# A low-rank update rewritten with counted semaphores, with a hardware loop on TensorE and other transfer sizes

## The chip, the cores and the metric

The kernel runs on one core of a Trainium2 chip. The metric is the device time of one launch in microseconds; less is better. The kernel before was run three times, 125.34 to 125.68 us, with a median of 125.58 us. One more execution was profiled.

## What is computed

```python
batch, seq, d_model, r = 16, 512, 768, 16
# x: 16 x 512 x 768 float32, A: 768 x 16, B: 16 x 768, scale 0.5
lora = np.matmul(np.matmul(x, A), B)
return (x + scale * lora).astype(np.float32)
```

Each of the 8,192 rows of x is multiplied by A down to 16 numbers and by B up to 768 again, and half of that is added to the row. x comes in once and goes out once in float32, 25.2 MB each way.

## The kernel before

A tile is 128 rows of x, one row to a partition; there are 64 tiles. They are moved in parts and computed in groups of 8, so there are 8 groups, numbered g. PARTS (line 13) gives the tiles of each part: 8, 8, 16, 16, 8, 8. Row by row a part is laid out so that a partition holds consecutive rows, and a transfer moves one contiguous piece for each of 128 partitions. ROOM (line 15) names four buffers; the last two parts use the buffers of the first two again. LOADS (line 17) splits the loads of parts 0 and 2 in halves of 4 and of 8 tiles. `loaded` (line 67) issues them.

All transfers of x go through SyncE's queue, in this order: loads of parts 0 to 3 at once, store of part 0, store of part 1, loads of parts 4 and 5 (each waits until the store that empties its buffer has landed), and the stores of parts 2 to 5, each when the last group of its part is added up (`finished`, line 157). A and B are small and go through ScalarE's queue (lines 89 and 90).

Before the first group, VectorE clears `a_rows` (line 87), turns A (line 98) and copies it into the block-diagonal weights `w_bd` (line 103), then copies B four times into `b_mm` (line 108). GpSimd clears `w_bd`, `b_mm` and `y_bd`.

A group takes these steps. `narrowed` (line 110) casts x to float16, four tiles on ScalarE and four on GpSimd, into one of two buffers `xh`. `turned` (line 116) transposes these in place on VectorE, in two instructions, in 32 x 32 blocks of 4-byte elements, so a pair of float16 values stays together. `projected` (line 123) multiplies by A on TensorE: 24 products into `ps_yt`. `spread` (line 134) scales the result and writes it into the block-diagonal `y_bd`, four instructions on ScalarE. `raised` (line 142) multiplies by B on TensorE, two tiles at a time, four products into one of two buffers `lora_ps`. `added` (line 152) adds these to x in place on VectorE, two tiles at a time, so four instructions a group.

The order on each engine is written out by hand (lines 167 to 194). For group g TensorE does `raised` 0 and 1, a third of `projected` of group g+1, `raised` 2, a third, `raised` 3, a third. VectorE does the two transposes of group g+1 and then the four adds of group g. ScalarE does the cast of group g+2 and then `spread` of group g+1. A framework puts the semaphores in; the program is straight-line code on every engine.

Of the kernel before, what the change touches and what calls it, by code (L numbers as in the profile page):

```python
# [9 lines left out]
MM_DT = mybir.dt.float16  # L10


PARTS = [8, 8, 16, 16, 8, 8]

ROOM = ["a", "b", "c", "d", "a", "b"]

LOADS = {0: [4, 4], 2: [8, 8]}


GROUP = 8  # L20

SUB = 4


@with_exitstack
def kernel(
    ctx: ExitStack,
    tc: tile.TileContext,
    x: bass.AP,
    A: bass.AP,  # L30
    B: bass.AP,
    scale: bass.AP,
    out: bass.AP,
):
    nc = tc.nc
    fp32 = mybir.dt.float32
    P = 128
    Q = 32

    x2 = x.flatten_outer_dims()  # L40
    out2 = out.flatten_outer_dims()
    T, D = x2.shape
    R = A.shape[1]
    NC = D // 64
    NG = sum(PARTS) // GROUP
    assert sum(PARTS) * P == T and NG * GROUP == sum(PARTS)
    sc = float(scale)

    const = ctx.enter_context(tc.tile_pool(name="const", bufs=1))
    xpool = ctx.enter_context(tc.tile_pool(name="xp", bufs=1))  # L50
    ypool = ctx.enter_context(tc.tile_pool(name="yp", bufs=1))
    ps_y = ctx.enter_context(tc.tile_pool(name="ps_y", bufs=2, space=bass.MemoryType.PSUM))
    ps_l = ctx.enter_context(tc.tile_pool(name="ps_l", bufs=2, space=bass.MemoryType.PSUM))

    parts = []
    where = []
    tok = 0
    for i, S in enumerate(PARTS):
        parts.append([None, tok, S])
        where += [(i, s) for s in range(S)]  # L60
        tok += S * P

    def rows(t2, i):
        _, tok0, S = parts[i]
        return t2[ds(tok0, S * P), :].rearrange("(p s) d -> p s d", s=S)

    def loaded(i):
        S = parts[i][2]
        t = xpool.tile([P, S, D], fp32, name=f"x_sb{i}", tag=ROOM[i])
        parts[i][0] = t  # L70
        end = 0
        for w in LOADS.get(i, [S]):
            nc.sync.dma_start(out=t[:, ds(end, w), :], in_=rows(x2, i)[:, ds(end, w), :])
            end += w

    a_rows = const.tile([Q, 64 * R], fp32, name="a_rows")
    a_t = const.tile([Q, 2, R, Q], fp32, name="a_t")
    b_f32 = const.tile([R, D], fp32, name="b_f32")  # L80
    w_bd = const.tile([P, NC, 2, P], MM_DT, name="w_bd")
    b_mm = const.tile([P, D], MM_DT, name="b_mm")
    xh = [const.tile([P, GROUP, D], MM_DT, name=f"xh{i}") for i in range(2)]
    y_bd = [const.tile([P, GROUP, P], MM_DT, name=f"y_bd{i}") for i in range(2)]

    ctx.enter_context(tc.manual_schedule())
    nc.vector.memset(a_rows, 0.0)  # L87
    loaded(0)
    nc.scalar.dma_start(out=b_f32, in_=B)
    nc.scalar.dma_start(out=a_rows[0:NC, :], in_=A.rearrange("(c e) r -> c (e r)", e=64))  # L90
    for i in range(1, 4):
        loaded(i)
    nc.gpsimd.memset(w_bd.rearrange("p c k m -> p (c k m)").bitcast(fp32), 0.0)  # L93
    nc.gpsimd.memset(b_mm.bitcast(fp32), 0.0)  # L94
    for t in y_bd:
        nc.gpsimd.memset(t.rearrange("p s m -> p (s m)").bitcast(fp32), 0.0)  # L96

    nc.vector.transpose(  # L98
        out=a_t.rearrange("i k r c -> i (k r) c"),
        in_=a_rows.rearrange("c (i k r) -> c (k r) i", k=2, r=R),  # L100
    )
    for b in range(P // Q):
        nc.vector.tensor_copy(  # L103
            out=w_bd[ds(b * Q, Q), :, :, ds(b * Q, R)],
            in_=a_t[:, :, :, 0:NC].rearrange("i k r c -> i c k r"),
        )
    for b in range(P // Q):
        nc.vector.tensor_copy(out=b_mm[ds(b * Q, R), :], in_=b_f32)  # L108

    def narrowed(g):  # L110
        for q in range(GROUP // SUB):
            i, s = where[g * GROUP + q * SUB]
            engine = nc.gpsimd.tensor_copy if q % 2 else nc.scalar.copy
            engine(out=xh[g % 2][:, ds(q * SUB, SUB), :], in_=parts[i][0][:, ds(s, SUB), :])  # L114

    def turned(g):
        for q in range(GROUP // SUB):
            v = xh[g % 2][:, ds(q * SUB, SUB), :].bitcast(fp32)
            nc.vector.transpose(out=v, in_=v)  # L119

    y_ps = {}

    def projected(g, steps):
        if g not in y_ps:
            y_ps[g] = ps_y.tile([P, GROUP, Q], fp32, name="ps_yt")
        xv = xh[g % 2].rearrange("p s (c j k) -> p s c j k", c=NC, k=2)
        for m in steps:
            c, k = divmod(m, 2)
            nc.tensor.matmul(  # L129
                y_ps[g], w_bd[:, c, k, :], xv[:, :, c, :, k],  # L130
                start=(m == 0), stop=(m == 2 * NC - 1),
            )

    def spread(g):
        y = y_ps.pop(g)
        for b in range(P // Q):
            q = ds(b * Q, Q)
            nc.scalar.mul(out=y_bd[g % 2][q, :, q], in_=y[q, :, :], mul=sc)  # L138

    lora = {}  # L140

    def raised(g, p):
        t = ps_l.tile([P, 2, D], fp32, name="lora_ps")
        lora[g, p] = t
        for h in range(2):
            lhsT = y_bd[g % 2][:, 2 * p + h, :]
            for n0, w in ((0, 512), (512, 256)) if h == 0 else ((0, 256), (256, 512)):
                nc.tensor.matmul(  # L148
                    t[:, h, ds(n0, w)], lhsT, b_mm[:, ds(n0, w)], start=True, stop=True
                )  # L150

    def added(g, p):
        i, s = where[g * GROUP + 2 * p]
        xs = parts[i][0][:, ds(s, 2), :]
        nc.vector.tensor_tensor(out=xs, in0=xs, in1=lora.pop((g, p)), op=mybir.AluOpType.add)  # L155

    def finished(g):
        i, s = where[g * GROUP + GROUP - 1]
        if s + 1 == PARTS[i]:
            nc.sync.dma_start(out=rows(out2, i), in_=parts[i][0])  # L160
            if i == 1:
                loaded(4)
                loaded(5)

    MMS = 2 * NC
    THIRD = MMS // 3
    narrowed(0)
    narrowed(1)
    turned(0)
    projected(0, range(MMS))  # L170
    spread(0)
    for g in range(NG):
        more = g + 1 < NG
        raised(g, 0)
        raised(g, 1)
        if g + 2 < NG:
            narrowed(g + 2)
        if more:
            turned(g + 1)
        added(g, 0)  # L180
        if more:
            projected(g + 1, range(0, THIRD))
        raised(g, 2)
        added(g, 1)
        if more:
            projected(g + 1, range(THIRD, 2 * THIRD))
        raised(g, 3)
        added(g, 2)
        if more:
            projected(g + 1, range(2 * THIRD, MMS))  # L190
        added(g, 3)
        finished(g)
        if more:
            spread(g + 1)


# [33 lines left out]
```

## Time and profile before

| | us |
|---|---|
| median of three runs | 125.58 |
| the profiled execution | 125.14 |
| its span, first to last instruction | 123.3 |
| VectorE busy | 89.8 |
| TensorE busy (products) | 51.8 |
| ScalarE busy | 35.3 |
| GpSimd busy | 25.1 |

The span is what the profile shows; the 1.8 us between it and the profiled time lie around it. A busy share is a mean over the span, so each engine must be looked at in the stage where it might be last. The profile's page cuts the span into 40 slices of 3.1 us and gives the busy tenths of each engine and of the 16 DMA engines that carry the transfers. Beneath the page's DMA rows the trace keeps a record for each packet, with its queue, its size, its start and its duration; where the text speaks of packet records, it means these.

A transfer that is issued is not under way yet: the DMA engines work through what one queue was given in order of issue. A store that is issued while earlier transfers are still moving costs nothing as long as it is there before the engines run out of work.

### The profile page before, as it was taken

Reading aid. Unit: us, or ns where it says so; the run is one execution under the profiler, and the core shown is the slowest. Engines: PE = TensorE matmul, PEld = TensorE weight load, DVE = VectorE, ACT = ScalarE, POOL = GpSimd, SP = SyncE. Lnnn points to the kernel's source line nnn. Section 1 sums busy time; section 2 is a strip of 40 time slices with the busy share of each in tenths; the row PEclk is TensorE's granted clock in tenths of the full one; section 3 lists DMA queues with packets and bytes.
Section 4 is the critical chain, followed back from the end, with each engine's and each line's share of the span. In section 5 each row is a group of like instructions: output and inputs, shape, how many; then the busy total and the mean of one; then the engine's idle time right before and its main releaser. Section 6 shows DMA issues by size and latency. Waiting matters only on the chain.

```text
span 123.3 us, 854 instructions
## 1 busy us (share of the span) xinstructions
PE 51.8 (42%) x320; PEld 32.3 (26%) x320; DVE 89.8 (73%) x58; ACT 35.3 (29%) x41; POOL 25.1 (20%) x16
## 2 busy tenths in 40 slices
PE   0000001948943844844794594484489432000000
PEld 0000001625622522532462362252246210000000
DVE  2019997826999999999989999999998499000000
ACT  1235007149094040849004084354000400000000
POOL 8101807135080000844000080350000000000000
PEclk9999999999999999999779999999977999555555
DMA  4999999999998897999999999989989989999980
GB/s 73 398 371 466 406 454 414 454 430 391 510 510 383 383 499 335 430 414 454 414 446 422 422 454 507 407 383 494 449 351 478 478 351 446 391 438 438 414 375 32
DMA packets 2075, 50.47 MB, mean 409 GB/s; under 512 B 252, under 2 KB 252, under 8 KB 280
## 3 DMA queue, kind: packets, MB, share of 16 engines
q1 hardware_dynamic: 2016, 50.33, 96.0%
q10 hardware_dynamic: 56, 0.10, 0.4%
q8 instruction: 2, 0.03, 0.1%
q14 instruction: 1, 0.01, 0.0%
HBM read 25.26 MB, written 25.17 MB: 409 GB/s over the span
## 4 chain that ended last, share of the span: by engine, by line
DVE 57%; PE 12%; issue 6%; DMA 5%; ACT 2%; DVEq 1%; ACTq 0%
DVE x_sb L155 31%; DVE xh L119 19%; PE ps_yt L129 8%; DMA a_rows<-in_A_dram 5%; PE lora_ps L148 5%; DVE w_bd L103 3%; ACT y_bd L138 2%; DVE b_mm L108 2%; DVE a_t L98 2%; DVEq L225 1%; DVE a_rows L87 1%; ACTq L225 0%; ACTq L138 0%; DVEq L103 0%; DVEq L98 0%
## 5 line engine op out<-in xcount | busy, mean ns | idle before, releaser
L155 DVE TENSOR_TENSOR x_sb<-x_sb,lora_ps 128x1536 f32<-128x1536 f32 x32 | 54.0, 1741 | 6.2 <-PE lora_ps L148 6.2
L129 PE MATMUL ps_yt<-xh,w_bd 128*128 128x256 f16 x192 | 28.8, 299 | 31.1 <-DVE xh L119 31.1
L148 PE MATMUL lora_ps<-b_mm,y_bd 128*128 128x512 f16 (+1 forms) x128 | 26.1, 338 | 19.7 <-ACT y_bd L138 13.8
L114 POOL CAST xh<-x_sb 128x3072 f16<-128x3072 f32 x8 | 22.2, 2781 | 56.2 <-DMA x_sb<-in_x_dram 49.7
L129 PEld LDWEIGHTS <-w_bd 128*128 128x128 f16 x192 | 20.2, 105 | 39.4 <-issue 33.3
L114 ACT CAST xh<-x_sb 128x3072 f16<-128x3072 f32 x8 | 22.0, 2752 | 23.8 <-DMA x_sb<-in_x_dram 23.7
L119 DVE STREAM_TRANSPOSE xh<-xh 128x1536 f32<-128x1536 f32 x16 | 27.4, 1754 | 1.0 <-ACT xh L114 1.0
L138 ACT ACTIVATE y_bd<-ps_yt 32x256 f16<-32x256 f32 x32 | 12.0, 375 | 35.9 <-PE ps_yt L129 35.3
L148 PEld LDWEIGHTS <-y_bd 128*128 128x128 f16 x128 | 12.1, 100 | 30.6 <-ACT y_bd L138 16.1
L98 DVE STREAM_TRANSPOSE a_t<-a_rows 32x1024 f32<-32x1024 f32 x1 | 1.9, 1931 | 6.9 <-DMA a_rows<-in_A_dram 6.9
L103 DVE CAST w_bd<-a_t 32x384 f16<-32x384 f32 x4 | 4.3, 1087 | 0.1
L108 DVE CAST b_mm<-b_f 16x768 f16<-16x768 f32 x4 | 2.2, 550 | 0.1
L114 ACT ACT_TABLE_LOAD x1 | 1.3, 1283 | 2.5 <-DVE a_rows L87 2.5
L87 DVE MEMSET a_rows<- 32x1024 f32 x1 | 0.9, 912 | 1.0 <-PEq L211 1.0
L93 POOL MEMSET w_bd<- 128x1536 f32 x1 | 1.4, 1379 | 0.3 <-POOLq L211 0.3
L96 POOL MEMSET y_bd<- 128x512 f32 x2 | 1.0, 528 | 0.0
L94 POOL MEMSET b_mm<- 128x384 f32 x1 | 0.4, 418 | 0.0
L211 POOL MEMSET const-float32-0.0<- 128x1 f32 x1 | 0.1, 100 | 0.2 <-issue 0.2
L211 POOL MEMSET const-bfloat16-1.0<- 128x1 bf16 x1 | 0.1, 103 | 0.0
L211 POOL MEMSET const-uint8-127<- 128x1 uint8 x1 | 0.1, 102 | 0.0
L211 POOL MEMSET const-float32-1.0<- 128x1 f32 x1 | 0.1, 100 | 0.0
## 6 DMA issues: line engine op xcount, KB each, us to landing
x_sb<-in_x_dram SPq DMA_DIRECT2D x5, 3072.0 KB, 20.9
out_dram<-x_sb SPq DMA_DIRECT2D x4, 3072.0 KB, 18.5
out_dram<-x_sb SPq DMA_DIRECT2D x2, 6144.0 KB, 24.7
x_sb<-in_x_dram SPq DMA_DIRECT2D x1, 6144.0 KB, 45.6
x_sb<-in_x_dram SPq DMA_DIRECT2D x2, 1536.0 KB, 9.1
b_f<-in_B_dram ACTq DMA_DIRECT2D x1, 48.0 KB, 4.0
a_rows<-in_A_dram ACTq DMA_DIRECT2D x1, 48.0 KB
```

The source lines that it names most:

```text
L87: nc.vector.memset(a_rows, 0.0)
L93: nc.gpsimd.memset(w_bd.rearrange("p c k m -> p (c k m)").bitcast(fp32), 0.0)
L98: nc.vector.transpose(out=a_t.rearrange("i k r c -> i (k r) c"), in_=a_rows.rearrange("c (i k r) -> c (k r) i", k=2, r=R),)
L103: nc.vector.tensor_copy(out=w_bd[ds(b * Q, Q), :, :, ds(b * Q, R)], in_=a_t[:, :, :, 0:NC].rearrange("i k r c -> i c k r"),)
L108: nc.vector.tensor_copy(out=b_mm[ds(b * Q, R), :], in_=b_f32)
L114: engine(out=xh[g % 2][:, ds(q * SUB, SUB), :], in_=parts[i][0][:, ds(s, SUB), :])
L119: nc.vector.transpose(out=v, in_=v)
L129: nc.tensor.matmul(y_ps[g], w_bd[:, c, k, :], xv[:, :, c, :, k], start=(m == 0), stop=(m == 2 * NC - 1),)
L138: nc.scalar.mul(out=y_bd[g % 2][q, :, q], in_=y[q, :, :], mul=sc)
L148: nc.tensor.matmul(t[:, h, ds(n0, w)], lhsT, b_mm[:, ds(n0, w)], start=True, stop=True)
L155: nc.vector.tensor_tensor(out=xs, in0=xs, in1=lora.pop((g, p)), op=mybir.AluOpType.add)
L225: with _tile.TileContext(nc) as tc:
```

## The change

The same steps are kept, with the same instructions on VectorE, ScalarE and GpSimd for each group. What differs:

- PARTS is 2, 6, 8, 16, 16, 16. The first three parts lie side by side in one buffer of 16 tiles, the next two in buffers of their own, and the last part comes into the first buffer again, in two loads of 8 tiles, and goes out in two stores of 8. Loads of 16 tiles are not split. The first cast on ScalarE, tiles 0 to 3, waits for the loads of 2 and of 6 tiles.
- The first reload waits for the stores of parts 0 and 1 together, the second for the store of part 2. Both early stores of parts 0 and 1 wait for group 0.
- Tile buffers and semaphores are allocated by hand. Each engine has a program of its own in a block; entering and leaving the block and the section around it adds instructions. At the end GpSimd waits for the last four stores and clears all semaphores, and then the closing sequence of before follows.
- The four copies into `b_mm` are on ScalarE, ahead of its first cast, and no longer on VectorE.
- ScalarE's order is `spread` of group g, then the cast of group g+2, which puts the same steps in the same sequence as before.
- VectorE has a drain after the four adds of a group, and the drain raises the count that SyncE's stores wait for.
- TensorE runs a hardware loop of four turns, two groups a turn (`h` is 0 and 1). A turn's first part raises the group before, so in the first turn four `raised` steps work on the cleared `y_bd`. What its waits take, they count down again (`take`), so each turn waits for the same values. The last group's four `raised` steps stand behind the loop.

```diff
-PARTS = [8, 8, 16, 16, 8, 8]
-ROOM = ["a", "b", "c", "d", "a", "b"]
-LOADS = {0: [4, 4], 2: [8, 8]}
+PARTS = [2, 6, 8, 16, 16, 16]
+ROOM = [(0, 0), (0, 2), (0, 8), (1, 0), (2, 0), (0, 0)]
...
+    LOADS = [(0, 0, 2), (1, 0, 6), (2, 0, 8), (3, 0, 16), (4, 0, 16), (5, 0, 8), (5, 8, 8)]
...
+    @block.sync
+    def _(e):
+        def store(i, s, n, done):
+            e.wait_ge(s_sum, sums_for(i, s, n))
+            e.dma_start(out=memory(out2, i, s, n), in_=held(i, s, n)).then_inc(done, 16)
+        load(LOADS[0])
+        for ld in LOADS[1:5]:
+            load(ld)
+        store(0, 0, 2, s_out0)
+        store(1, 0, 6, s_out0)
+        store(2, 0, 8, s_out1)
+        e.wait_ge(s_out0, 32)
+        load(LOADS[5])
+        e.wait_ge(s_out1, 16)
+        load(LOADS[6])
+        store(3, 0, 16, s_out)
+        store(4, 0, 16, s_out)
+        store(5, 0, 8, s_out)
+        store(5, 8, 8, s_out)
+    def narrowed(e, copy, done, g, q):
+        t = g * GROUP + q * SUB
+        for s in dict.fromkeys(load_sem(t + k) for k in range(SUB)):
+            e.wait_ge(s, 16)
+        if g >= 2:
+            e.wait_ge(s_y, g - 1)
+        copy(
+            out=xh[g % 2][:, ds(q * SUB, SUB), :], in_=held(*where[t], SUB)
+        ).then_inc(done, 1)
+    @block.scalar
+    def _(e):
+        e.dma_start(out=b_f32, in_=B).then_inc(s_b, 16)
+        e.wait_ge(s_ready, 1)
+        e.dma_start(
+            out=a_rows[0:NC, :], in_=A.rearrange("(c e) r -> c (e r)", e=64)
+        ).then_inc(s_a, 16)
+        e.wait_ge(s_zero, 1)
+        e.wait_ge(s_b, 16)
+        for b in range(NQ):
+            last = e.copy(out=b_mm[ds(b * Q, R), :], in_=b_f32)
+        last.then_inc(s_bm, 1)
...
+        narrowed(e, e.copy, s_nact, 0, 0)
+        narrowed(e, e.copy, s_nact, 1, 0)
+        for g in range(NG):
+            spread(g)
+            if g + 2 < NG:
+                narrowed(e, e.copy, s_nact, g + 2, 0)
+    @block.vector
...
+        turned(0)
+        for g in range(NG):
+            if g + 1 < NG:
+                turned(g + 1)
+            for p in range(PAIRS):
+                xs = held(*where[g * GROUP + 2 * p], 2)
+                e.wait_ge(s_lora, (g + 1) * PAIRS + p + 1)
+                e.tensor_tensor(
+                    out=xs, in0=xs, in1=lora[p % 2], op=mybir.AluOpType.add
+                ).then_inc(s_free, 1)
+            e.drain().then_inc(s_sum, 1)
+    @block.tensor
+    def _(e):
+        def take(s):
+            e.wait_ge(s, 1)
+            e.sem_inc(s, -1)
...
+        def raised(h, p):
+            if p == 0:
+                take(s_spread)
+            take(s_free)
...
+        with e.Fori(0, NG // 2):
+            for h in range(2):
+                raised(1 - h, 0)
+                raised(1 - h, 1)
+                projected(h, range(0, THIRD))
+                raised(1 - h, 2)
+                projected(h, range(THIRD, 2 * THIRD))
+                raised(1 - h, 3)
+                projected(h, range(2 * THIRD, MMS))
+        for p in range(PAIRS):
+            raised(1, p)
+    programs.close()
+    nc.gpsimd.wait_ge(s_out, 4 * 16)
...
+    nc.gpsimd.sem_clear(range(nums[0], nums[0] + len(nums)))
+    section.close()
```

## The prediction

> **What bounds the kernel now.** I read the page first (busy shares, slices, DMA queues), then the windows view for the DMA share stage by stage, then SyncE's queue (when each transfer is issued, what it waited for), and last the order of time on VectorE.
>
> ```profile
> span 123.3 us, 854 instructions
> ...
> PE 51.8 (42%) x320; PEld 32.3 (26%) x320; DVE 89.8 (73%) x58; ACT 35.3 (29%) x41; POOL 25.1 (20%) x16
> ...
> DMA  4999999999998897999999999989989989999980
> ...
> q1 hardware_dynamic: 2016, 50.33, 96.0%
> ...
> q8 instruction: 2, 0.03, 0.1%
> ```
>
> VectorE is the busiest compute engine at 73%, and the chain of waits runs over it. But the DMA row reads 9 in nearly every slice, and the one queue that carries x in and out takes 96.0% of 16 engines' span. The windows view says the same (columns: stretch, length, busy of PE, PEld, DVE, ACT, POOL, clock, DMA share, GB/s):
>
> ```profile
> 34.00:42.00 8.00, 3.94 (x27) 2.61 (x28) 8.00 (x5) 4.25 (x5) 2.75 (x1) 1.00 1.04 449
> ...
> 79.50:94.00 14.50, 9.81 (x60) 6.18 (x60) 14.50 (x9) 3.76 (x5) 2.33 (x1) 0.89 1.01 434
> ...
> 109.00:116.00 7.00, 0.00 (x0) 0.00 (x0) 0.00 (x0) 0.00 (x0) 0.00 (x0) 0.50 1.03 442
> ```
>
> A share of 1 means that all 16 engines are moving data, also after 105 us, when no compute is left. So the span is 1.75 us until the first data packet, 120.4 us of packets, and 1.17 us after the last (122.17). In the trace's packet records a 24,576-byte packet takes 912 ns and a 49,152-byte one 1815: 8 ns a packet plus 0.0368 ns a byte. For 1/16 of 50.33 MB in 112 packets that is 116.5 us; the other 3.9 us are start, small transfers and stragglers. VectorE sets the time only if a transfer is issued after its queue has run empty:
>
> ```profile
> 56.77 0.34 SPq L73 DMA_DIRECT2D x_sb<-in_x_dram  x1
> ...
> 66.10 0.34 SPq L160 DMA_DIRECT2D out_dram<-x_sb  x1
> ...
> 86.05 0.34 SPq L160 DMA_DIRECT2D out_dram<-x_sb  x1
> ...
> 96.71 0.33 SPq L160 DMA_DIRECT2D out_dram<-x_sb  x1
> ...
> 105.15 0.33 SPq L160 DMA_DIRECT2D out_dram<-x_sb  x1
> ```
>
> In the packet records the first engine is through with the work queued ahead of these stores at 76.3, 90.8, 105.3 and 112.6 us. Issue to first packet took 1.0 us for the first load (0.74 to 1.75). So the stores have 9.2, 3.7, 7.6 and 6.4 us to spare; the tightest is the second, part 3 of before.
>
> **The change, part by part.** *Transfers.* The queue still gets 14 transfers of 128 rows, in the same sequence: 48 tiles in, 16 out, 16 in, 16, 16, 8, 8 out. Sizes differ: 2+6 tiles for 4+4 and 16 for 8+8. By 8 ns a packet this is nothing: 14 x 8 packets on each engine in both. The reload's first half now waits for stores 0 and 1 together, 8 tiles, landing when store 0 of before did (56.65), so it is issued at about 56.8 with store 2's 7.3 us of packets as cover; without that cover it costs 1.0 us. Value 0, bounds 0 and 1.0.
>
> *VectorE's start.* Four b_mm copies leave VectorE (15.25, 2.24 us) for ScalarE, which was idle from 3.8 to 8.3. ScalarE's first cast now waits for 8 tiles, as GpSimd's did (11.88), not 4 (8.32).
>
> ```profile
> 8.79 1.93 DVE L98 STREAM_TRANSPOSE a_t<-a_rows 32x1024 f32<-32x1024 f32 x1 [6.87 <-DMA a_rows<-in_A_dram]
> ...
> 15.25 2.24 DVE L108 CAST b_mm<-b_f 16x768 f16<-16x768 f32 x4
> ...
> 28.80 6.75 DVE L155 TENSOR_TENSOR x_sb<-x_sb,lora_ps 128x1536 f32<-128x1536 f32 x4 [3.42 <-PE lora_ps L148]
> ...
> 34.03 2.75 POOL L114 CAST xh<-x_sb 128x3072 f16<-128x3072 f32 x1 [4.69 <-PE ps_yt L129]
> ...
> 38.82 6.71 DVE L155 TENSOR_TENSOR x_sb<-x_sb,lora_ps 128x1536 f32<-128x1536 f32 x4
> ```
>
> The first transposes can start at 15.25 for 17.52, and the first adds at 26.5 for 28.80. If A lands up to 2.3 us later behind the new 6-tile load, that gain is gone. Either way it is lost at group 2: its cast waits for all 16 tiles of part 3, the 32nd tile, which landed at 33.23 by the packet records, where before it needed the 24th (26.59). On ScalarE spread(1) is queued behind that cast. So: cast 33.5 to 36.3, VectorE's two transposes to 39.8 (3.43), adds of group 1 from 39.8 for 38.82. VectorE then runs 1.0 us late at 10.0 us a group (48.79 to 58.77), with the two slow-clock stalls. Group 5's store, 86.05, goes to about 87.1, still 2.7 us ahead of 89.8. Value 0.
>
> *TensorE.* The loop body keeps the order of products; 16 products of zeros run before the first group, while TensorE idled until 21.1. Its separate semaphore steps (51 ns each in the trace, 6 a group, 0.3 us) lie in the 2.0 us it waits for ScalarE each group. The drain after each group's adds comes just ahead of the store's issue and spends some of the 2.7 us. Value 0; without the cover 8 x 0.3 = 2.4 us.
>
> *Instruction fetches.* The row "q8 instruction" is two packets of 16,384 bytes, at 45.50 and 76.45, 1069 and 1099 ns long, each on a DMA engine that also moves x. The packets behind them took 506 and 363 ns longer than 1815, so a fetch sets one engine back 1.5 us. The engine with the first is the last of all, 122.17; without it, 120.6. Next come the one with the second, 121.45, and one that had slow packets but no fetch, 121.34; the rest end between 119.9 and 120.7. [...] One fetch late: that engine ends at 120.2 + 1.5 = 121.7, so -0.45; no fetch, no straggler: -1.5; both fetches, 0.
>
> *Front and end.* No row shows the added steps, so bounds. SyncE has a no-op, a wait for it and a taken branch ahead of its first load: three steps at 65 ns (122.526 to 122.591 in the closing rows) is 0.2; below, 0.1 if two overlap; above, 0.4 at 120 ns each (barrier, 0.536 to 0.656). At the end SyncE's wait for the stores becomes GpSimd's, then a clear of semaphores (96 ns), a hand-over to SyncE and back (33 + 42 ns), four steps at 65: 0.43; below 0.2; above 0.8, the whole closing sequence (122.53 to 123.33) again.
>
> [...]
>
> **The sum**, against the profiled execution: span 123.33 + 0.2 + 0.43 - 0.45 = 123.5; with the 1.8 us around the span (125.14 - 123.33), 125.3. That is 0.2 above the profiled 125.14. The median of the runs is 125.58, 0.44 above the profiled one, so on its scale 125.7.
>
> **The rivals.** *A, the fetches were the price and go.* For it: the last engine to finish is the one with the first fetch. Against it: a third engine ends at 121.34 without any. If none falls in the span and no straggler takes the place: 125.58 + 0.2 + 0.43 - 1.5 = 124.7.
>
> [...]
>
> *C, a store comes late.* If VectorE falls 2.7 us further back by group 5, the DMA queue runs dry at 91 us. For it: the two stalls at the halved clock (61 and 92 us) cost 2 us each, and their place may move. Against: before has 3.7 us to spare there with both in. At 4 us more: 125.58 + 0.2 + 1.3 = 127.1, less what it overlaps with the straggler, 126.6.
>
> **How the numbers follow.** Within 0.3%, or 0.38 us, is about what a measurement of this kernel can tell from no change. Forecast 125.7 at 0.50, own range 125.3 to 125.9; A 0.20; B 0.15; C 0.15. A is faster, B and C slower: 0.20, 0.50, 0.30. The range reaches to A's 124.7 less 0.1, and up past the high ends of front and closing without a gain (125.58 + 0.4 + 0.8 = 126.8) and C to 127.3, leaving out most of B.
>
> **What would show it.** Right: DMA share near 1 from 3 to 121 us, first load issued near 0.95, the last data packet near 121.9, 1.6 us from it to the end, VectorE's second group of adds near 39.8 and its last near 106. Wrong: gaps in the DMA row near 56 or 91 us, more than two packets on the instruction queue, or a first load later than 1.2 us.

## The result, and the profile after

| | before | changed |
|---|---|---|
| median of 18 runs | 125.33 us | 124.83 us |
| profiled execution | 125.14 us | 124.72 us |
| its span | 123.3 us | 122.9 us |

The ratio is 0.9969, with a 95% interval of 0.9954 to 0.9984. Two more series on other chips gave 0.9983 (0.9964 to 1.0001) and 0.9959 (0.9937 to 0.9980). So the change makes the kernel about 0.3% faster, some 0.4 us, where no change was forecast. The page of the changed kernel, in the lines that answer to those shown of before:

```profile
span 122.9 us, 965 instructions
...
PE 54.2 (44%) x336; PEld 32.2 (26%) x336; DVE 85.6 (70%) x54; ACT 38.6 (31%) x45; POOL 25.0 (20%) x16
...
DMA  2999995995997996999999999999899899799990
...
q1 hardware_dynamic: 2016, 50.33, 96.0%
...
q14 instruction: 2, 0.02, 0.0%
```

The transfers fill the span as before. The 5s in the DMA row are a matter of counting: the row and the windows view put a packet's whole time where the packet begins, so that a thin slice stands beside a full one. By the packet records all 16 engines are busy throughout the slices with a 5. The row that is missing is the one to see: there is no "q8 instruction" any more, so no packet of 16,384 bytes fell into this span. It still comes: the packet records have it at 124.01 us, behind the last instruction at 122.9. The two on q14 have 8,192 bytes; before had one of that kind in its span, at 89.1 us. Such a packet takes 0.31 us and the one behind it was 0.1 to 0.5 us over its size; the two engines ended at 121.01 and 121.24, ahead of the last one at 121.45. Now VectorE in order of time, and the one row of ScalarE that it waits for:

```profile
14.53 3.44 DVE L214 STREAM_TRANSPOSE xh<-xh 128x1536 f32<-128x1536 f32 x2 [2.41 <-ACT xh L150]
...
26.59 6.75 DVE L224 TENSOR_TENSOR x_sb<-x_sb,lora_ps 128x1536 f32<-128x1536 f32 x4 [1.38 <-PE lora_ps L255]
36.30 3.44 DVE L214 STREAM_TRANSPOSE xh<-xh 128x1536 f32<-128x1536 f32 x2 [2.96 <-ACT xh L150]
39.66 3.38 DVE L224 TENSOR_TENSOR x_sb<-x_sb,lora_ps 128x1536 f32<-128x1536 f32 x2
```

```profile
33.52 2.75 ACT L150 CAST xh<-x_sb 128x3072 f16<-128x3072 f32 x1 [8.07 <-DMA x_sb<-in_x_dram]
```

The first adds start 2.2 us earlier than before (26.59 for 28.80), and then VectorE waits 2.96 us for ScalarE's cast, which waits for the load of 16 tiles. Group 1's adds start 0.8 us later than before (39.66 for 38.82). SyncE's queue:

```profile
0.94 2.77 SPq L123 DMA_DIRECT2D x_sb<-in_x_dram  x5
33.42 13.67 SPq L127 DMA_DIRECT2D out_dram<-x_sb  x3
55.52 7.93 SPq L123 DMA_DIRECT2D x_sb<-in_x_dram  x2
67.17 38.94 SPq L127 DMA_DIRECT2D out_dram<-x_sb  x4
```

The first load is issued 0.2 us later than before. The last four stores are issued at 67.17, 87.59, 97.80 and 105.78, each 0.6 to 1.5 us later than before and still ahead of the end of the work in the queue.

The stretches of the two profiled executions, by the packet records and the instruction records:

| us | before | changed | difference |
|---|---|---|---|
| span's start to the first load's issue | 0.74 | 0.945 | +0.2 |
| from there to the first packet of x | 1.01 | 1.03 | 0 |
| first to last packet of x | 120.43 | 119.48 | -0.95 |
| last packet to the span's end | 1.16 | 1.50 | +0.34 |

The gain lies in the third row alone, and part of it is given back in the first and the last. What lies around the span is 1.8 us in both of these executions.

### The profile page after: what moved, and what is told of

The parts are those of the page before. It is cut to its first block, busy times and chain, and to the rows that moved or that the text cites. A ratio compares the mean times of both kernels' runs of the same rounds, so it can differ in the third digit from the quotient of the medians.

```text
span 122.9 us, 965 instructions
## 1 busy us (share of the span) xinstructions
PE 54.2 (44%) x336; PEld 32.2 (26%) x336; DVE 85.6 (70%) x54; ACT 38.6 (31%) x45; POOL 25.0 (20%) x16
## 5 line engine op out<-in xcount | busy, mean ns | idle before, releaser
L255 PE MATMUL lora_ps<-b_mm,y_bd 128*128 128x512 f16 (+1 forms) x144 | 31.0, 352 | 37.4 <-PEq L233 37.4
L241 PE MATMUL ps_yt<-xh,w_bd 128*128 128x256 f16 x192 | 27.1, 285 | 11.8 <-PEq L233 11.8
L255 PEld LDWEIGHTS lora_ps<-b_mm,y_bd 128*128 128x128 f16 x144 | 13.3, 103 | 50.6 <-issue 44.8
L241 PEld LDWEIGHTS ps_yt<-xh,w_bd 128*128 128x128 f16 x192 | 18.9, 100 | 20.1 <-issue 14.8
L174 ACT CAST b_mm<-b_f 16x768 f16<-16x768 f32 x4 | 3.3, 829 | 0.0
L204 DVE CAST w_bd<-a_t 32x384 f16<-32x384 f32 x4 | 1.9, 472 | 0.1
```

The source lines that it names most:

```text
L174: last = e.copy(out=b_mm[ds(b * Q, R), :], in_=b_f32)
L204: last = e.tensor_copy(out=w_bd[ds(b * Q, Q), :, :, ds(b * Q, R)], in_=a_t[:, :, :, 0:NC].rearrange("i k r c -> i c k r"),)
L241: last = e.matmul(y_ps[h], w_bd[:, c, k, :], xv[:, :, c, :, k], start=(m == 0), stop=(m == MMS - 1),)
L255: last = e.matmul(t[:, k, ds(n0, w)], y_bd[h][:, 2 * p + k, :], b_mm[:, ds(n0, w)], start=True, stop=True,)
```

## The experiments

Each kernel is the changed one with one edit. Times of single executions scatter by 0.2 to 0.3 us, spans by 0.1 to 0.2, so the mean span of a series is given beside the ratio to the kernel before on the same chip. The changed kernel's mean span was 122.99 (18 executions), 123.05 (12) and 122.90 (8) on three chips; the kernel before had 123.2 to 123.5.

**TensorE's loop written out.**

```diff
-        with e.Fori(0, NG // 2):
+        for _ in range(NG // 2):
```

> The changed kernel with TensorE's loop written out, so that its stream grows from 240 to 751 instructions; nothing else differs. Theory (instruction fetches in the span set single DMA engines back 1.5 us each, and the last engine sets the end): two or three packets of 16,384 bytes appear on the instruction queue inside the span, the engines that carry them end 1.2 to 1.6 us later than their neighbours, and the time is 0.5 to 0.9 us above the changed kernel, so 1.000 to 1.004 of the kernel before. Rival (the gain comes from the new transfer sizes or from VectorE's earlier start): the time stays at 0.997 of the kernel before, whatever is fetched.

Measured: 1.0163 (1.0141 to 1.0185), mean span 124.32. The profile has two packets of 16,384 bytes, at 45.24 and 87.42 us. The engine with the first ended last, at 122.64 us, 2.4 us behind the typical engine; the one with the second ended at 121.43. More came than was expected: 1.3 us in the span, and the time around the span was 2.55 us for 1.8. The rival falls.

The packet records say where the 0.7 us around the span belong: a third packet of 16,384 bytes lies behind the last instruction, at 125.84 us. Five of the profiles have one there (two of the changed kernel, this one, and two of kernels below), and in each the packet's end, counted from the span's start, is the execution's time plus 0.23 to 0.24 us. The time around the span is 1.8 to 2.55 us in these five and 1.8 to 1.9 in the others. This suggests that a fetch behind the span still lengthens the time; no run tests that by itself.

**One fetch late in the span.**

```diff
         for p in range(PAIRS):
             raised(1, p)
+        for _ in range(200):
+            e.wait_ge(s_w, 1)
```

> The changed kernel with 200 waits on a count that is already there, placed behind TensorE's last product; they end about 110 us and nothing waits for them but the barrier that opens long before the last store lands. They only lengthen TensorE's stream by 100 instructions. Theory: one packet of 16,384 bytes on the instruction queue between 103 and 111 us, one DMA engine 1.5 us later than without it, ending near 121.9 to 122.3 against 121.4, and the time up by 0.3 to 0.8 us. Rival (what counts is the number of instructions run, or the loop, not the fetch): no change from the changed kernel within 0.2 us.

Measured: 0.9998 (0.9982 to 1.0015), mean span 123.19. The packet came, at 109.13 us. The price is 0.2 us over the changed kernel's mean span and, by the ratio, 0.2 to 0.5 us over its three series, which were on other chips; the low end of what was expected is not excluded. In the profile the fetch did not set the end: its engine ended at 121.42, ahead of one at 121.67 that had slow packets and no fetch. So a fetch this late matters little, and what it costs is not settled.

**The loop moved by 100 places, first try.**

```diff
         e.wait_ge(s_w, 1)
         e.wait_ge(s_bm, 1)
+        for _ in range(200):
+            e.wait_ge(s_w, 1)
         with e.Fori(0, NG // 2):
```

> The changed kernel with 200 such waits ahead of TensorE's loop, where TensorE idles until 12.5 us anyway. [...]

Measured: 1.019 (1.0137 to 1.0243), but not because the loop had moved. The waits stand behind the wait for the weights, so they ran after it, at 106 ns each, and TensorE began at 23.6 us for 12.5. VectorE came late all the way, and the store of part 4 was issued at 93.29, after the queue had run empty. The windows view shows it (columns as above: DMA share is the last but one):

```profile
84.00:91.00 7.00, 4.53 (x32) 2.78 (x31) 7.00 (x5) 1.87 (x1) 0.41 (x1) 1.00 0.97 421
91.00:94.30 3.30, 1.44 (x12) 0.85 (x11) 3.16 (x3) 1.50 (x4) 0.00 (x0) 1.00 0.64 271
94.30:104.00 9.70, 5.37 (x38) 3.24 (x37) 9.13 (x6) 1.50 (x4) 0.00 (x0) 1.00 0.94 405
```

The share drops to 0.64 between 91.0 and 94.3; counted packet by packet it is 0.22 there, and most engines stood still for 2.1 to 3.1 us. This execution took 128.56 us, more than the quickest two (126.43 and 126.46), so only its gap is used. It is the prediction's rival C, made by hand. One packet of 16,384 bytes came, at 105.76 us, so the loop did not fetch once a turn; but as TensorE ran late, its place was tested again.

**The same, without delaying TensorE.**

```diff
+        for _ in range(180):
+            e.wait_ge(s_spread, 1)
         e.wait_ge(s_w, 1)
         e.wait_ge(s_bm, 1)
```

> The changed kernel with 180 waits on a count that is already there, ahead of TensorE's first wait for the weights, where it idles until 12.5 us: 90 instructions of 106 ns, done near 11 us. They move the loop by 90 places without delaying it. In the run that put such waits behind that wait, TensorE began 11 us late, group 5's store came when the queue had been empty for 3 us, and only one packet of 16,384 bytes fell in the span. Theory: with TensorE on time the queue never runs empty, one or two such packets, 0.9995 to 1.004. [...]

> The same kernel as the one with 90 instructions ahead of TensorE's loop, whose executions fell into two lots, three with spans of 122.9 to 123.2 and nine of 124.4 to 124.9; the one that was profiled was of the lower lot and had a single packet of 16,384 bytes, at 78.4 us. Theory (fetches): an execution of the upper lot has an engine that carries such a packet earlier, before 76 us, or carries two, and ends 1.4 us later for it. Rival (a store comes late): a gap in the DMA row before a store, as where TensorE began 11 us late.

Measured: 1.0056 (1.0027 to 1.0085) and, again, 1.0088 (1.0057 to 1.0119). The first series fell into two lots, three executions with spans up to 123.2 us and nine from 124.4; in the second, one was of the lower lot. The first profile is of the lower lot: one packet of 16,384 bytes at 78.44 us, its engine at 121.49, the span 122.9. The second is of the upper lot: one such packet at 30.92 us, its engine at 123.07, the span 124.4. The ratios lie above the theory's 1.004; the count of packets, one in each profile, is within its one or two. The second page:

```profile
span 124.4 us, 1055 instructions
...
DMA  2999996998899698999999999998997998999960
...
q8 instruction: 1, 0.02, 0.1%
```

By the packet records the engines are busy throughout from 3 to 118 us, so no store came late; what differs is when the one fetch came. It did not come once a turn. But in both profiles it came behind a jump back of the loop: the jump before 30.92 us was at 30.19, and the one before 78.44 was at 74.60, after which TensorE waited until 77.6. So it is not excluded that a jump called for that one fetch.

**One turn written out, three in the loop.**

```diff
-        with e.Fori(0, NG // 2):
+        def turn():
             for h in range(2):
...
+        turn()
+        with e.Fori(0, NG // 2 - 1):
+            turn()
```

> The changed kernel with the first of the loop's four turns written out ahead of a loop of three. TensorE does the same in the same order; its stream grows from 240 to 412 instructions, and what it runs until 60 us is as in the kernel with all four turns written out, where a packet of 16,384 bytes came at 45.2 us. Theory (a fetch in mid-span costs its DMA engine 1.5 us, and 0.6 to 1.2 us more at the turn from loads to stores near 76 us, as the engines with such a fetch showed in the kernel before and in the written-out one): one such packet near 45 us, that engine the last of all, and a span 0.7 to 1.3 us above the changed kernel's 123.0 (mean of 30 executions). Rival (only fetches late in the span or their number count): below 0.3 us.

Measured: 1.0061 (1.0037 to 1.0086), mean span 124.13, 1.1 above the changed kernel's. One packet of 16,384 bytes, at 45.44 us, as in the written-out kernel:

```profile
q8 instruction: 1, 0.02, 0.1%
```

```profile
119.50:121.50 2.00, 0.00 (x0) 0.00 (x0) 0.00 (x0) 0.00 (x0) 0.00 (x0) 0.50 0.20 86
121.50:123.00 1.50, 0.00 (x0) 0.00 (x0) 0.00 (x0) 0.00 (x0) 0.00 (x0) 0.50 0.04 16
```

The windows show what a straggler looks like: for packets that begin between 119.5 and 121.5 us the share is 0.20, and for those that begin later only 0.04, which is less than one engine of 16. That one engine holds up the whole kernel to 122.83; the next ended at 121.41. This is the cleanest dose: the same work in the same order, one fetch in mid-span, and 1.1 us. Expected was 0.7 to 1.3.

The engines with a fetch, each followed through the packet records by linking a packet to the one that ended when it began (a packet of 49,152 bytes takes 1815 ns, one of 24,576 takes 912):

| kernel | fetch at, us | it took, ns | the packet behind it, ns over its size | its packet of 24,576 near 76 us, ns | engine ends at, us |
|---|---|---|---|---|---|
| shifted, again | 30.92 | 1069 | +499 | 2325 | 123.07 |
| written out | 45.24 | 1098 | +469 | 2144 | 122.64 |
| one turn out | 45.44 | 1069 | +499 | 2040 | 122.83 |
| before | 45.50 | 1069 | +506 | 1499 | 122.17 |
| before | 76.45 | 1099 | +363 | 914 | 121.45 |
| shifted | 78.44 | 934 | +400 | 1074 | 121.49 |
| written out | 87.42 | 966 | +378 | 1007 | 121.43 |

A fetch ahead of 76 us costs its engine 1.6 us at once and 0.6 to 1.4 us more at 76. There the queue turns from loads to stores. The other engines finish their last load packet, and the one that is behind has one load packet more than they; the packet that it is moving at that moment, its last but one, is the long one, and the last takes 912 ns again. Not every late engine is late by a fetch: where TensorE began 11 us late, two engines without one in mid-span had a packet of 2158 and 1942 ns there. And engines that are not late lose a little: in the changed kernel's profile the last load packet of each engine took 0.1 to 0.7 us too long, in that of before none of the others did by more than 0.02.

A fetch after 76 us costs 1.3 to 1.5 us and puts its engine where another engine ends in any case: each of these profiles has an engine with six or more packets some 50 to 100 ns too long and no fetch, which ends at 121.3 to 121.4.

**The transfer sizes of before.**

```diff
-PARTS = [2, 6, 8, 16, 16, 16]
+PARTS = [8, 8, 16, 16, 8, 8]
...
+    LOADS = [
+        (0, 0, 4), (0, 4, 4), (1, 0, 8), (2, 0, 8), (2, 8, 8), (3, 0, 16), (4, 0, 8), (5, 0, 8)
+    ]
```

> The changed kernel with the parts, loads and stores of the kernel before (4+4, 8, 8+8, 16 tiles in; 8, 8 out; 8, 8 in; 16, 16, 8, 8 out); the rest as changed. Theory (the sizes do nothing): the same time as the changed kernel within 0.2 us, 0.996 to 0.998 of the kernel before, though group 2's cast starts near 27 instead of 33.5 us and VectorE ends about 1 us earlier. Rival (the sizes gave the gain): back to 1.000 of the kernel before, or above it by the 0.5 us that front and closing cost.

> The changed kernel with the parts, loads and stores of the kernel before, and with the waits of the last group's four raised steps not counted down, so that TensorE's stream is 4 instructions shorter (236). The run with these sizes alone had one packet of 16,384 bytes at 103.7 us, three instructions from TensorE's end, and 0.9995. Theory (fetches, not sizes): with the stream shorter the fetch falls behind the end of the span, and the time is that of the changed kernel, 0.996 to 0.998. If the fetch is still there, 0.999 to 1.000. Rival (the sizes): 0.999 to 1.000 without a fetch in the span.

Measured: 0.9995 (0.9982 to 1.0008), mean span 122.92, and for the shorter stream 0.9983 (0.9968 to 0.9999), mean span 123.21. Both profiles had one late fetch (103.72 and 98.48 us), so the second did not take it away as was meant. By the ratios the first agrees with the rival, but its span, 122.92, is that of the changed kernel, and on its chip the kernel before had 123.21. Each is best set beside its partner on the same chip, with the new sizes: 0.9995 beside 0.9998 for the late fetch, both with one such packet in the profile, and 0.9983 beside 0.9983 for the changed kernel. The sizes account for nothing that can be seen; a part below 0.2 us is not excluded.

**A and B on SyncE's queue.**

```diff
         load(LOADS[0])
+        e.wait_ge(s_ready, 1)
+        e.dma_start(
+            out=a_rows[0:NC, :], in_=A.rearrange("(c e) r -> c (e r)", e=64)
+        ).then_inc(s_a, 16)
+        e.dma_start(out=b_f32, in_=B).then_inc(s_b, 16)
```

> The changed kernel with A and B loaded through SyncE's queue, between the load of 2 tiles and that of 6, and no longer through ScalarE's. In the packet records of the changed kernel the 16 packets of B took 121 to 1045 ns among the packets of x, those of A 159 to 173, and the packets of x behind A's took 1065 to 1152 ns where their size would give 685. Theory (two queues that share an engine cost it some 0.4 to 0.6 us each time): in one queue A and B cost 0.3 us an engine and the packets of x keep their pace, so the last data packet comes 0.4 to 0.7 us earlier and the time falls to 0.992 to 0.994 of the kernel before. Rival (the slow packets are a start-up of the engines, whoever comes second): no change within 0.2 us from the changed kernel. A lands near 5 us for 8.2, which nothing waits for.

Measured: 1.013 (1.0108 to 1.0153), mean span 124.94; the theory is wrong. Packets of 18,432 bytes behind A took 833 to 1688 ns where 685 is their size, worse than with two queues; at 45 us nearly all engines had one of 2133 to 2718 for 1815; and three engines ended between 122.7 and 123.5. There was no fetch of 16,384 bytes in the span. Why three engines fell behind is not settled.

**The changed kernel beside these, and two loads ahead of the section.** The second of these kernels issues the loads of 2 and 6 tiles right behind the opening barrier:

```diff
+    early = early_loads(nc, args[0])
     with _tile.TileContext(nc) as tc:
...
-        load(LOADS[0])
-        for ld in LOADS[1:5]:
+        for ld in LOADS[2:5]:
```

> The changed kernel as it is, on the same chip as the runs beside it. Theory and rival alike: about 0.997 of the kernel before, since that is what it was. It is there so that the others can be compared on one chip: what adds one late fetch (200 waits behind TensorE's last product) gave 0.9998.

> The changed kernel with the loads of 2 and of 6 tiles issued ahead of the hand-written section, right behind the opening barrier, and no longer behind the no-op and the branch that open it. The first load should then be issued near 0.73 us for 0.945. The other engines enter the section about 0.9 us later, so A lands later, which nothing waits for until group 2's load. Theory (the DMA engines are busy from the first packet to the last, so a start 0.2 us earlier is an end 0.2 us earlier): a span of 122.8 for 123.0. Rival (the last engine is set by stragglers, not by the start): no change.

> The changed kernel as it is, beside the version with two loads ahead of the section, on one chip. A span of 123.0 and 0.997 to 0.998 of the kernel before.

> The version with the loads of 2 and 6 tiles ahead of the section once more, on the same chip as the changed kernel. Theory (the start of the transfers shifts the end one for one): a mean span 0.2 to 0.4 us below that of the changed kernel beside it. Rival (the 122.6 of its first 12 executions came from the chip): the same span within 0.1.

Measured: the changed kernel 0.9983 and 0.9959, as above; its profile in the last series had one fetch, at 108.30 us, and a span of 123.1, so in some executions the fetch falls just inside the span. The version with early loads: 0.9961 (0.9937 to 0.9986) with a mean span of 122.60, then, beside the changed kernel, 0.9937 (0.9915 to 0.9960) and 122.58 for 122.90.

```profile
0.74 0.86 SPq L304 DMA_DIRECT2D x_sb<-in_x_dram  x2
1.87 1.67 SPq L124 DMA_DIRECT2D x_sb<-in_x_dram  x3
```

The first load is issued at 0.74 us again, as before the change, and the span is 0.32 us shorter, somewhat more than the 0.2 us by which the load comes earlier; why is not shown. The rival falls. This version is the best measured here.

## Why the prediction was wrong

**What bounds the kernel** was read rightly. The DMA engines are busy from the first packet to the last; 0.2 us less ahead of the first load is 0.3 us less at the end; and where a store came late, the time went up.

**Transfers** were right at 0, within the 0.2 us that the two kernels with the old sizes leave open. **VectorE's start** was right in its steps: first adds at 26.5 forecast and 26.59 seen, ScalarE's cast for group 2 at 33.5 and 33.52, group 1's adds at 39.8 and 39.66. That the last adds end near 106 (105.7 seen) is partly luck. The drains make a group 10.2 us instead of 10.0, and the two stalls at a slow clock, which the forecast carried along, were not there: the windows view has a clock of 1.00 over 58 to 68 and 90 to 100 us, where before had 0.83. Group 5's store was put at 87.1 and came at 87.59, so the drains ate half a microsecond of the room, as the prediction allowed for.

**Front and end** were right in kind: 0.2 forecast and seen ahead of the first load; at the end 0.43 forecast, 0.34 seen.

**Instruction fetches** is the step that failed: the term of -0.45 was mis-sized, because of where it put the fetch that remains and what it took that fetch to cost. It held that one fetch late in the span would remain, that it would set its engine at 121.7, and took -0.45 from before's 122.17. No run shows that term: that one fetch would come late could not be told ahead, since the same stream had its fetch at 108.30 us in one profile and behind the end of the span in two others. What was measured in its place is -0.95, the stretch from first to last packet. In the profiled execution the packet came behind the last instruction, and the end was set by an engine with slow packets and no fetch, at 121.45. Where a fetch does come late in the span, its engine still ends at 121.3 to 121.7, level with that straggler, and the stretch from first to last packet is 119.5 to 119.7 us (five profiles with a fetch at 98 to 109 us and a queue that never ran empty), which is 0.7 to 0.9 below before's. So the term was too small with such a fetch and without one.

The fetch of before at 45.5 us was also priced too low, at 1.5 us, what it costs on the spot. The same engine's packet at 76.2 us took 1499 ns for 912, so by these numbers it would have ended near 120.0 without the fetch, an estimate, and not at 120.6. This does not enter the sum, but with it an engine with a fetch in mid-span loses 2.2 to 3.0 us in all, where the prediction had 1.5.

With what was measured in the two profiles the sum is 123.33 + 0.2 - 0.95 + 0.34 = 122.92, the span of the profile, as it must be, since the stretches fill the span; that the -0.95 belongs to the fetches rests on the engine that ended last before and on the experiments that put a fetch back. Of the 0.9 us between 125.7 and 124.83, this term makes 0.5, the end 0.1, and some 0.25 come from the scale: three runs of before had a median of 125.58, eighteen have 125.33.

**Rival A** (the fetches were the price and go) is what happened in the span, though one fetch went only as far as behind it. Its worked time of 124.7 came out near the measured one by luck: it had a stretch shorter by 1.5, which was too much, since the straggler of 121.4 took the place that the prediction warned of, and it started from the 125.58 that was 0.25 too high.

**Rival B** (the loop fetches once a turn, and is slower for it) did not happen. The changed kernel has no fetch in its span, and the kernels with the loop moved by 90 places and with one turn written out show one fetch each, not one a turn. That a loop should fetch on its jumps was the author's assumption, and no run shows it; none here has a longer loop.

**Rival C** (a store comes late) did not happen in the changed kernel. The kernel that began TensorE 11 us late shows its mechanism and where it starts: the store of part 4 issued at 93.29 us left engines idle, the same store at 87.59 did not.

## What to carry to other kernels

Where the DMA engines are busy from end to end, as here, the time is that of the last of 16 engines: 122.17 us in a span of 123.3 before, 121.45 in 122.9 after. An instruction fetch that landed on one engine ahead of 76 us set that engine back by 1.6 us, and by 0.6 to 1.4 more where the queue turned from loads to stores; with one turn of the loop written out that was 1.1 us of the span. Late in the span it cost little, because another engine ended as late (with a fetch at 109.13 us its engine ended at 121.42, another without one at 121.67). The kernel with TensorE's work in a loop had either no such fetch in its span or a late one, though the loop changes nothing in what the engine computes; but moving the loop by 90 places brought an early one back (at 30.92 us), so the place of the code has to be measured and not reckoned. What a section adds ahead of the first transfer shows at the end (0.2 us there, 0.3 us in the span), so transfers that need nothing from the section belong ahead of it.

## What the runs showed of the hardware

An instruction fetch took the time of a DMA engine that also moved data: the packet of 16,384 bytes took 0.93 to 1.1 us of it, and the data packet behind it 0.36 to 0.51 us more than its size.

An engine that fell behind by 1.6 us did not only stay behind: the load packet that it was moving when the others turned to stores took 1.5 to 2.3 us for 0.91. Why it slowed is not shown, and engines that were late without a fetch had it too.

A separate wait on TensorE for a count that was already there took 106 ns, with two of the program's waits in one instruction, and ran in order behind a wait that was not met: with 100 of them behind the wait for the weights TensorE began at 23.6 us for 12.5.

When the fetch came differed from execution to execution: with one and the same program it came at 78.44 us in one profile and at 30.92 in another, and with it the span moved by 1.5 us. What decides it is not shown.
